# A hybrid decoder layer: later work on the decay rows, and transposes set one to three steps apart

## The chip, the cores and the metric

The kernel runs on one core of a Trainium2 chip. The metric is device time in microseconds (us): before the change the median of three runs is 1289.85 us (1289.18 to 1289.87).

## The reference, cut to what matters

One decoder layer works on 1024 prompt tokens and 32 sample tokens (8 sequences of 4). One input projection feeds two groups of heads, a gated delta rule (4 heads of width 128, chunks of tokens) and sliding-window attention; their outputs are joined, projected, normalised, sent through a SwiGLU block and normalised again. The change touches the delta rule and the keys of the attention:

```python
decay = jnp.exp(jnp.where(causal, gc[..., :, None] - gc[..., None, :], -jnp.inf))
A = jnp.where(strict, jnp.einsum('bnhid,bnhjd->bnhij', kb, kc) * decay, 0.0)
M = A + jnp.eye(C, dtype=A.dtype)
sol = lax.linalg.triangular_solve(M, rhs, left_side=True, lower=True, unit_diagonal=True)
u, w = sol[..., :DV], sol[..., DV:]
...
v_new = u_n - jnp.einsum('bhcd,bhde->bhce', w_n, S)
S = S * gl_n[..., None, None] + jnp.einsum('bhcd,bhce->bhde', kd_n, v_new)
```

## The kernel before, in words

Everything is stored transposed: features lie on the 128 partitions, tokens run along the free axis. The tokens are worked in two parts, s = 0 (tokens 0 to 511) and s = 1 (tokens 512 to 1023 and the 32 sample tokens, 544 columns). For each part `mix_in` (L1452) runs 22 dense tiles of the input projection: 4 for the keys of the delta heads, one for the attention keys (`kb`), one for the values, 4 for the attention queries, 4 each for the delta queries and values, 4 for the gates. A dense product (L426) is three float32r matmuls for each of 8 input blocks (high and low halves of both factors). For s = 0 it runs on 512 columns at once, for s = 1 in two groups of 272. Its weights are split on ScalarE (L162) and VectorE (L163). After both parts comes the output projection, `out_proj(0)` on 512 columns and `out_proj(1)` on two groups of 272, then the normalisation and the SwiGLU block.

All work beside the dense products is written as Python generators: `decay`, `delta_k`, `keys`, `attn`, `inverse`, `recur`, `sample_delta` and others. The program writes dense matmuls, and after every half tile it runs one round (`unit`, L422, and `pump`, L287) over the list of living generators, in the order in which they were started; each advances to its next `yield`. A yield carries a cost in ns of TensorE time, and a round ends when the sum reaches a budget of 2750 (3000 in the output projection). A round is called a step here. `idle(n)` (L321) lets n steps pass. A few generators (`sample_attn`, `sample_delta`) also advance in short rounds between.

That order is not yet the order on the engines. The program is built with `schedule_with_timeline_sim=True` (L2092): at build time each engine's queue is filled from the instructions that the builder takes to be ready at that time, the one written first going first; splits of weights and evacuations of dense products (`high_priority`) go ahead of all. So an instruction whose inputs are taken to be there can move ahead of its place when its engine has nothing else, and one that is written later loses its place to others that are ready. Dense matmuls are nearly always ready, so on TensorE a step's work stays at its step.

The steps of the second part are numbered here from the one in which the four `decay(1, h)` issue their loads (step 0). Every group of 272 columns ends one step: the key tile of head 3 ends with step 1, `kb` with 3, `vb` with 5, the attention queries with 7, 9, 11 and 13, the delta queries with 15 to 21, the values with 23 to 29, the gates with 31, 33, 35 and 37. The 8 tiles of `out_proj(0)` take two steps each, 38 to 53. Counted through the code, the generators that the change touches stand so:

- `decay(s, h)` (L586) loads a head's rows of decays and of beta from DRAM to all partitions (L598, L601), rests 9 steps (L603), adds a mask (L604, step 9), takes the exponential (L608, step 10) and multiplies (L610, step 11).
- `delta_k(s, h)` (L650) transposes the keys and forms their products in two PSUM banks (L662, L664); it squares the keys on ScalarE (L668), whose last one frees the first bank; the second is held until the decay rows are ready (L674 to L679). There are four such banks (tag `ms`). Heads 0 to 2 hold three of them from their transposes to step 11, and head 3, which needs two, makes its transposes then, in step 11, and is done in step 12.
- `inverse(s)` (L706) starts when all four heads are done (step 12). It moves 32x32 blocks to DRAM and back (L714, L717), inverts 64 of them at once by a loop of 31 columns on GpSimd (L726, L728, written until step 20), moves them back (L732, L739), rests 4 steps (L743), transposes three blocks on VectorE (L746, step 24) and then joins blocks by small matmuls: L754 and L755 in step 25, L765 to L768 in 26, L783 in 27, L797 in 28.
- `keys(s)` (L974) for s = 1 copies the sample keys on GpSimd (L987), waits one yield, and transposes keys (L992, L993) in step 7.
- `delta_w` (L847) needs the inverse: L852 and L857, from step 29 on. `recur(1)` (L867) needs all of it: four chunks of two steps each (L887 to L892, L904 and L906), steps 33 to 40, then the output transposes L947 in 42 and 43. `sample_delta` transposes the sample tokens' output (L1396) after that, in step 45, and adds the state products (L1427). `gate` (L1160) multiplies with the gates, and `split_mix` (L1771) splits the result, which `out_proj(1)` needs.

For s = 0 a step is half a tile of 512 columns, and the same generators run alike.

Of the kernel before, what the change touches and what calls it, by code (L numbers as in the profile page):

```python
# [87 lines left out]
IDLE = (9, 4, 2, 3, 2, 4)  # L88
# [120 lines left out]
def _program(k):  # L209
# [14 lines left out]
    def page(shape, dt, name, tag="hp"):  # L224
        assert room(tag), (tag, name)
        live[tag] += 1
        t = (k.fp if tag == "xp" else k.hp).tile([shape[0], HW_], dt, tag=tag, bufs=cap[tag], name=name)
        w = int(np.prod(shape[1:]))
        G.memset(t[:, 0:1].bitcast(F32), 0.0)
        v = t[:, :w]  # L230
        return v if len(shape) == 2 else v.rearrange("p (a b) -> p a b", b=shape[2])
# [15 lines left out]
    def bank(tag="ms"):  # L247
        assert room(tag)
        live[tag] += 1
        return k.pa.tile([P, 512], F32, tag=tag, bufs=cap[tag], name=tag)  # L250
# [6 lines left out]
    def drop(tag="hp", n=1):  # L257
        live[tag] -= n
        assert live[tag] >= 0
# [4 lines left out]
    def small(shape, name, bufs=1, dt=F32):  # L264
        return k.sp.tile(shape, dt, tag=name, bufs=bufs, name=name)
# [4 lines left out]
    def bc(ap, shape):  # L270
        return ap.broadcast_to(shape)
# [41 lines left out]
    def wait(*names):  # L313
        while not all(n in flags for n in names):
            yield BLOCK

    def have(tag, n=1):
        while not room(tag, n):
            yield BLOCK

    def idle(n):  # L321
        for _ in range(n):
            yield 0.0
# [262 lines left out]
    def decay(s, h):  # L586

        yield from wait(("g", s))
        if s:
            yield from wait(("E", 0))  # L590
        yield from have("hp")
        if s not in Bm:
            Bm[s] = small([P, 16, P], "Ball")
        Ball = Bm[s]
        g = gat[s]
        R = page([P, 4, P], F32, f"R{s}{h}")
        gd = g["dram"]
        dma(out=R.rearrange("p n t -> p (n t)"),  # L598
            in_=gd[h * 4:h * 4 + 4, :].rearrange("n t -> (n t)").partition_broadcast(P))
        RB = Ball[:, h * 4:h * 4 + 4, :]  # L600
        dma(out=RB.rearrange("p n t -> p (n t)"),  # L601
            in_=gd[16 + h * 4:16 + h * 4 + 4, :].rearrange("n t -> (n t)").partition_broadcast(P))
        yield from idle(IDLE[0])  # L603
        V.tensor_tensor(R, R, bc(C["rmask"].unsqueeze(1), [P, 4, P]), ALU.add)  # L604
        yield 0.0
        for n in range(4):
            c = h * 4 + n
            A.activation(R[:, n, :], R[:, n, :], AF.Exp, bias=g["ngc"][:, c:c + 1])  # L608
        yield 0.0
        V.tensor_tensor(RB, RB, R, ALU.mult)  # L610
        Rt[s, h] = R
        flags.add(("R", s, h))
        yield 0.0
# [92 lines left out]
    def inverse(s):  # L706
# [37 lines left out]
        for q in range(3):  # L744
            o = 32 * (q % 2)
            V.transpose(Dl[32 * q:32 * q + 32, :, o:o + 32], Eall[32 * q:32 * q + 32, :, 32 * q:32 * q + 32])  # L746
        yield 0.0
        yield from have("ms")
        yield from have("hp")
# [224 lines left out]
    def keys(s, kb):  # L974
        yield from have("hp", 4)
        kh = [page([P, 512], F32R, f"kh{s}{i}") for i in range(2)]
        kl = [page([P, 512], F32R, f"kl{s}{i}") for i in range(2)]
        for i in range(2):
            a, o = slice(64 * i, 64 * i + 64), slice(64 - 64 * i, 128 - 64 * i)
            A.copy(kh[i][a, :], kb[a, 0:512])  # L980
            A.copy(kh[i][o, :], kb[a, 0:512])
            V.tensor_tensor(kl[i][a, :], kb[a, 0:512], kh[i][a, :].bitcast(F32), ALU.subtract)
            V.tensor_tensor(kl[i][o, :], kb[a, 0:512], kh[i][a, :].bitcast(F32), ALU.subtract)
            yield 0.0
        at[s, "k"] = (kh, kl)
        if s:
            G.tensor_copy(ksT, kb[:, 512:544])  # L987
            yield 0.0
            yield from have("ms")
            yield from have("hp")  # L990
            pt = bank()
            tr(pt[:, 0:P], kb[:, 384:512], ident)  # L992
            tr(pt[0:32, P:2 * P], kb[:, 512:544], ident)  # L993
            kp = page([P, 2, P], F32, "kp")
            V.tensor_copy(kp[:, 0, :], pt[:, 0:P])
            V.tensor_copy(kp[0:32, 1, :], pt[0:32, P:2 * P])
            drop("ms")
            dma(out=O["k_p"], in_=kp[:, 0, :])
            dma(out=O["k_s"][:, 124:128, :], in_=kp[0:32, 1, :])
            drop()  # L1000
            dma(out=O["k_s"][:, 0:124, :], in_=I["cache_k"][:, 4:128, :])
            dma(out=O["v_s"][:, 0:124, :], in_=I["cache_v"][:, 4:128, :])
        drop()
        flags.add(("keys", s))
        yield 300.0
# [446 lines left out]
    def mix_in(s, before_last):  # L1452
# [6 lines left out]
        for h in range(4):  # L1459
            spawn(decay(s, h))  # L1460
        spawn(delta_k(s, 0, pre))
        for h in range(1, 4):
            spawn(delta_k(s, h, conv_dense(s, h, 4 + h)))
        spawn(norms_k(s))
        spawn(inverse(s))
        spawn(keys(s, kv_dense(s, 12, "kb")))
        spawn(vals(s, kv_dense(s, 13, "vb")))
        for m in range(4):
# [635 lines left out]
```

## Time and profile before

| | us |
|---|---|
| median of 3 runs | 1289.85 |
| the profiled execution: device time | 1288.69 |
| its span, first to last instruction | 1286.8 |
| TensorE (PE) busy | 1248.8 |
| VectorE (DVE) busy | 871.9 |
| ScalarE (ACT) busy | 616.2 |
| GpSimd (POOL) busy | 395.9 |

Times in the profile are us from the start of the span. A row of the timeline gives the start, the duration, engine, line, operation, what is written and read, the shape and how many follow each other; in square brackets, how long the engine had been idle before, and what ended that. PE is the matmuls and PEld the loads of their weights. A matmul's duration runs past the start of the next one, so the distance of two starts is its price. SP issues the transfers.

### The profile page before, as it was taken

Reading aid. Unit: us, or ns where it says so; the run is one execution under the profiler, and the core shown is the slowest. Engines: PE = TensorE matmul, PEld = TensorE weight load, DVE = VectorE, ACT = ScalarE, POOL = GpSimd, SP = SyncE. Lnnn points to the kernel's source line nnn. Section 1 sums busy time; section 2 is a strip of 40 time slices with the busy share of each in tenths; the row PEclk is TensorE's granted clock in tenths of the full one; section 3 lists DMA queues with packets and bytes.
Section 4 is the critical chain, followed back from the end, with each engine's and each line's share of the span. In section 5 each row is a group of like instructions: output and inputs, shape, how many; then the busy total and the mean of one; then the engine's idle time right before and its main releaser. Section 6 shows DMA issues by size and latency. Waiting matters only on the chain.

```text
span 1286.8 us, 24943 instructions
## 1 busy us (share of the span) xinstructions
PE 1248.8 (97%) x8701; PEld 1127.1 (88%) x8701; DVE 871.9 (68%) x1873; ACT 616.2 (48%) x1374; POOL 395.9 (31%) x1207
## 2 busy tenths in 40 slices
PE   9998999999999999996999999999999999999996
PEld 7887789999989888985999999999999998888995
DVE  6696975788885679868956655555655765622674
ACT  7674744757746433686322222322324554522453
POOL 1009411205722144437633433222332112201210
PEclk9999999999999999998999999999999999999999
DMA  7432341332133646444444422222324886733461
GB/s 252 138 90 70 93 133 39 104 120 83 45 116 105 193 140 205 157 155 155 167 155 141 147 92 74 76 83 75 112 86 119 295 269 190 214 100 114 143 218 47
DMA packets 119102, 170.81 MB, mean 133 GB/s; under 512 B 20272, under 2 KB 50096, under 8 KB 118960
## 3 DMA queue, kind: packets, MB, share of 16 engines
q1 hardware_dynamic: 118976, 169.22, 41.7%
q8 instruction: 68, 1.11, 0.3%
q14 instruction: 58, 0.48, 0.1%
HBM read 138.44 MB, written 31.75 MB: 132 GB/s over the span
## 4 chain that ended last, share of the span: by engine, by line
PE 48%; DVE 2%; DMA 1%; ACT 0%; issue 0%; DVEq 0%; SPq 0%; ACTq 0%; POOL 0%; POOLq 0%
PE acc L1990 6%; PE acc L1988 6%; PE acc L1989 6%; PE acc L1821 5%; PE acc L1819 5%; PE acc L1820 5%; PE ms L1819 5%; PE ms L1821 5%; PE ms L1820 5%; DMA hr<-hd 1%; DVE y L1554 1%; DVE wl L163 0%; PE ms L1522 0%; DMA wr<-in_w_ffo_t 0%; PE ms L1497 0%
## 5 line engine op out<-in xcount | busy, mean ns | idle before, releaser
L163 DVE TENSOR_TENSOR wl<-wr,wh 128x512 fp32r<-128x512 f32 x330 | 238.1, 725 | 141.0 <-ACT wh L162 131.6
L162 ACT CAST wh<-wr 128x512 fp32r<-128x512 f32 x330 | 197.2, 602 | 266.4 <-PE acc L1989 104.3
L433 PE MATMUL acc<-xh,wh 128*128 128x272 f32 (+1 forms) x528 | 174.5, 330 | 0.6 <-ACT qsm L1045 0.4
L434 PE MATMUL acc<-xl,wh 128*128 128x272 f32 (+1 forms) x528 | 173.7, 329 | 0.5 <-DVE xl L347 0.5
L435 PE MATMUL acc<-xh,wl 128*128 128x272 f32 (+1 forms) x528 | 173.6, 329 | 0.2 <-DVE wl L163 0.2
L1990 PE MATMUL acc<-hx,wl 128*128 128x272 f32 (+1 forms) x528 | 171.5, 325 | 1.5 <-DVE wl L163 1.4
L1988 PE MATMUL acc<-hx,wh 128*128 128x272 f32 (+1 forms) x528 | 171.8, 326 | 0.0
L162 ACT CAST wh<-S 128x512 fp32r<-128x512 f32 x88 | 54.4, 619 | 148.8 <-PE acc L1820 89.7
L1990 PEld LDWEIGHTS acc<-hx,wl 128*128 128x128 f32 x528 | 99.2, 188 | 10.6 <-DVE wl L163 2.4
L434 PEld LDWEIGHTS acc<-xl,wh 128*128 128x128 f32 x528 | 100.4, 190 | 8.9 <-issue 2.4
L433 PEld LDWEIGHTS acc<-xh,wh 128*128 128x128 f32 x528 | 100.4, 190 | 8.5 <-issue 1.0
L435 PEld LDWEIGHTS acc<-xh,wl 128*128 128x128 f32 x528 | 100.4, 190 | 8.0 <-issue 1.0
L1988 PEld LDWEIGHTS acc<-hx,wh 128*128 128x128 f32 x528 | 99.2, 188 | 8.2 <-issue 0.2
L1989 PE MATMUL acc<-hx,wh 128*128 128x272 f32 x352 | 101.5, 288 | 0.2 <-DVE hx L1718 0.2
L163 DVE TENSOR_TENSOR wl<-S,wh 128x512 fp32r<-128x512 f32 x88 | 72.2, 823 | 37.7 <-ACT wh L162 34.9
L1989 PE MATMUL acc<-hy,wh 128*128 128x512 f32 x176 | 69.4, 394 | 0.0
L1989 PEld LDWEIGHTS acc<-hx,wh 128*128 128x128 f32 x352 | 66.7, 189 | 0.7 <-DVE hx L1718 0.4
L433 PE MATMUL acc<-mh,wh 128*128 128x272 f32 (+1 forms) x192 | 64.0, 333 | 0.0
L434 PE MATMUL acc<-ml,wh 128*128 128x272 f32 (+1 forms) x192 | 63.3, 330 | 0.0
L435 PE MATMUL acc<-mh,wl 128*128 128x272 f32 (+1 forms) x192 | 63.1, 329 | 0.0
L1717 ACT CAST hx<-hr 128x272 fp32r<-128x272 f32 (+1 forms) x66 | 31.7, 486 | 46.1 <-DMA hr<-hd 41.5
L1659 POOL TENSOR_TENSOR S<-wr,S 128x512 f32<-128x512 f32 x22 | 34.8, 1581 | 53.4 <-DVE wl L163 53.4
(631 smaller groups left out, 3481.0 us busy)
## 6 DMA issues: line engine op xcount, KB each, us to landing
wr<-in_w_ffo_t SPq DMA_DIRECT2D x120, 256.0 KB, 3.0
wr<-in_w_ffi_t SPq DMA_DIRECT2D x108, 256.0 KB, 2.7
wr<-in_w_in_t SPq DMA_DIRECT2D x88, 256.0 KB, 2.6
wr<-in_w_out_t SPq DMA_DIRECT2D x32, 256.0 KB, 3.3
hd<-x SPq DMA_DIRECT2D x22, 272.0 KB, 2.7
hr<-hd SPq DMA_DIRECT2D x44, 136.0 KB, 2.8
hd<-x SPq DMA_DIRECT2D x22, 256.0 KB, 2.0
hr<-hd SPq DMA_DIRECT2D x22, 256.0 KB, 5.1
```

The costliest lines, as they stand in the source:

```text
L162: nc.scalar.copy(hi, raw)
L163: nc.vector.tensor_tensor(lo, raw, hi.bitcast(F32), ALU.subtract)
L433: mm(ps[:, :cw], wh, xh[kt][:, c0:c0 + cw], start=(kt == 0), stop=False)
L434: mm(ps[:, :cw], wh, xl[kt][:, c0:c0 + cw], start=False, stop=False)
L435: mm(ps[:, :cw], wl, xh[kt][:, c0:c0 + cw], start=False, stop=(kt == n - 1))
L1659: G.tensor_tensor(t["S2"], W.get(r["A12"]), t["S2"], ALU.subtract)
L1819: mm(o, wh[:, kt, :], xh, start=(start and kt == 0), stop=False, **kw)
L1820: mm(o, wh[:, kt, :], xl, start=False, stop=False, **kw)
L1821: mm(o, wl[:, kt, :], xh, start=False, stop=(kt == 3), **kw)
L1988: mm(ps, wh[:, f % 4, :], xh, start=(f == 0), stop=False)
L1989: mm(ps, wh[:, f % 4, :], xl, start=False, stop=False)
L1990: mm(ps, wl[:, f % 4, :], xh, start=False, stop=(f == NF - 1))
```

## The change: what it does

```diff
@@ decay
-        yield from idle(IDLE[0])
+        yield from idle(IDLE[0] + 5 * s)
@@ inverse
             V.transpose(Dl[32 * q:32 * q + 32, :, o:o + 32], Eall[32 * q:32 * q + 32, :, 32 * q:32 * q + 32])
+            yield 0.0
         yield 0.0
@@ keys, for s = 1
             G.tensor_copy(ksT, kb[:, 512:544])
-            yield 0.0
+            yield from idle(3)
             yield from have("ms")
```

Three edits. In the second part the work on the decay rows rests 14 steps instead of 9. In both parts the three block transposes of the inverse stand in three steps instead of one, and with the yield that follows them the matmuls that use them come three steps later. In the second part the key transposes come two steps later. No instruction is added or taken away.

## The prediction, made before the change ran

> **What bounds the kernel now.** The page first: the sum over the engines says which of them can be late.
>
> ```profile
> span 1286.8 us, 24943 instructions
> PE 1248.8 (97%) x8701; PEld 1127.1 (88%) x8701; DVE 871.9 (68%) x1873; ACT 616.2 (48%) x1374; POOL 395.9 (31%) x1207
> ```
>
> TensorE is idle for 1286.8 - 1248.8 = 38 us. The edits add and remove no instruction, so they can only change this idle time and what follows from it. The waits of PE come next (who waited, for whom, us in total, times, longest):
>
> ```profile
> PE ms L992 <- ACT junk L668: 2.3, 1, 2.3
> PE ms L754 <- DVE hs L699: 2.0, 1, 2.0
> PE ms L1427 <- DVE S L1432: 1.5, 2, 0.9
> PE acc L433 <- ACT qsm L1045: 0.4, 1, 0.4
> PE ms L755 <- DVE Dl L746: 0.3, 1, 0.3
> ```
>
> Two of these stand at places the change touches: the key transpose L992 and the first joining product of the inverse, L754. Then the stretches around them (length, then busy us of PE, PEld, DVE, ACT, POOL, granted clock, DMA share, GB/s):
>
> ```profile
> 260.00:270.00 10.00, 7.73 (x51) 7.50 (x50) 7.32 (x18) 6.82 (x22) 0.10 (x1) 0.83 0.69 225
> 350.00:360.00 10.00, 8.05 (x107) 7.54 (x105) 9.21 (x26) 5.81 (x20) 0.20 (x2) 0.83 0.69 172
> 480.00:490.00 10.00, 8.53 (x68) 6.72 (x65) 10.00 (x18) 3.01 (x6) 4.38 (x14) 0.97 0.28 84
> 490.00:500.00 10.00, 10.00 (x66) 9.52 (x65) 9.27 (x25) 2.25 (x5) 3.62 (x42) 0.85 0.91 264
> ```
>
> Each wait costs twice: idle time (2.27 us in the first stretch, 1.95 in the second) and then a clock of 0.83 over the 10 us, about 0.17 x 10 = 1.7 us of lost speed. So each place holds about 3.7 to 4.0 us. The last two rows are the end of the second part, where the last state products hold up TensorE: 10 - 8.53 = 1.47 us and 0.18 x 10 = 1.8 us of clock.
>
> **Part 1, the key transposes two steps later.** TensorE's own order at the wait, then what VectorE and ScalarE did (rows of the timeline):
>
> ```profile
> 249.81 0.29 PE L435 MATMUL acc<-xh,wl 128*128 128x272 f32 x1
> 249.93 0.29 PE L433 MATMUL acc<-xh,wh 128*128 128x272 f32 x1
> ...
> 260.71 0.29 PE L433 MATMUL acc<-xh,wh 128*128 128x272 f32 x1
> 263.27 0.33 PE L992 MATMUL ms<-cst,kb 128*128 128x128 f32 x1 [2.27 <-ACT junk L668]
> ...
> 264.79 0.43 PE L433 MATMUL acc<-xh,wh 128*128 128x272 f32 x1
> ```
>
> ```profile
> 261.54 0.69 DVE L604 TENSOR_TENSOR R<-R,cst 128x512 f32<-128x512 f32 x1 [5.98 <-DMA R<-gd]
> 262.26 0.43 DVE L1042 SCALAR_TENSOR_TENSOR qs<-acc,qs 64x272 fp32r<-64x272 f32 x1
> ```
>
> ```profile
> 262.27 0.69 ACT L608 ACTIVATE R<-R,gt 128x128 f32<-128x128 f32 x2 [4.59 <-DVE R L604]
> 262.87 0.26 ACT L668 ACTIVATE junk<-ms 128x128 f32<-128x128 f32 x1
> ...
> 275.45 0.20 ACT L1045 ACTIVATE qsm<-acc 128x32 f32<-128x32 f32 x1 [1.06 <-DVE qs L1042]
> ```
>
> The chain reads backwards: L992 wants the bank that the last L668 frees; ScalarE has L608 in front of it, L608 waits for L604, and L604 holds VectorE for 5.98 us because the decay rows have not landed. A group of 24 matmuls, 0.12 us apart, is 3.0 us, so two steps are about 6 us: at 260.7 + 6 = 267 the bank has been free since 263.1 and L992 waits for nothing. The value transpose L1015, a step later than L992 was, meets it at 263.7. This wait goes.
>
> But VectorE and ScalarE stay where they are, and the first group's L1042, behind L604 in its queue, was held too. The evacuations of the first query tile end with L1045 at 275.45 + 0.20, and PE already waits for that one (0.4, the fourth row of the waits). If it arrives 3.7 us sooner, it waits that much longer there. So part 1 alone gives nothing. The bounds: -4.0 us if VectorE's order moves in its favour, +0.5 if the later wait slows the clock longer.
>
> **Part 2, five more steps before the decay work.** Does it move L604, which is the root?
>
> ```profile
> L598 SPq DMA_DIRECT2D R<-gd x8: 326/382/1179, 48.8 to 260.9; - x8
> L604 DVE TENSOR_TENSOR R<-R,cst x8: 669/692/693, 52.9 to 268.5; 128x512 f32<-128x512 f32 x8
> ```
>
> In the first part L604 starts 4.1 us after the first load was issued, although nine steps, each of 12 matmuls or at least 1.4 us, stand between them in the code. It has moved ahead to an idle VectorE, and more steps cannot hold what nine did not. So I keep the stall of 5.98 us and cost this edit at nothing here; were L604 held instead, part 1 would give its 4.0 us.
>
> What it does move is TensorE's work behind it. Heads 0 to 2 keep their banks, in the code's count, to step 16 instead of 11, so head 3's transposes go to step 16, the inverse starts in step 17 and not 12, its loop is written until step 25 and its rest lasts to 29. Attention of the first two heads gets its banks in step 16 too, one or two steps late, and is done before step 24, so nothing that ends the part waits for it.
>
> **Part 3, three steps for the block transposes.** With them L754 goes from step 25 to 33, and the later products from 26, 27, 28 to 34, 35, 36. What it waited for:
>
> ```profile
> 284.81 0.38 PE L664 MATMUL ms<-kT 128*128 128x128 f32 x2
> ```
>
> ```profile
> 297.10 1.12 DVE L677 SCALAR_TENSOR_TENSOR Ball<-ms,hs,Ball 128x128 f32<-128x128 f32 x4
> ...
> 355.26 0.70 DVE L746 STREAM_TRANSPOSE Dl<-Eall 32x512 f32<-32x512 f32 x1 [0.63 <-DMA Eall<-ed]
> ```
>
> ```profile
> 305.51 0.23 POOL L726 TENSOR_TENSOR itmp<-Db,Ab 64x31 f32<-64x31 f32 x1 [1.83 <-DMA Ab<-bd]
> ```
>
> ```profile
> 349.10 0.51 SPq L732 DMA_DIRECT2D ed<-Db  x1
> ```
>
> ```profile
> 356.02 0.24 PE L754 MATMUL ms<-Dl,Ball 32*32 32x32 f32 x2 [1.95 <-DVE hs L699]
> ...
> 358.46 0.26 PE L755 MATMUL ms<-Dl,Ball 32*32 32x32 f32 x1
> ```
>
> The data path is L664, L677 12.3 us later, the loop on GpSimd from 305.5 to 349.1, two transfers, L746. Five steps put L664 some 15 us later, and the data at most as much, since L677 and the loop find no more work in front of them: 355.3 + 15 = 370, the last transpose 2.2 us after. TensorE comes to L754 eight steps later, at least 8 x 3.0 = 24 us, at 378 or after. So it finds the data there with 6 us to spare. Gain: 1.95 of idle and, between 1.4 (8.05 of 10 us busy at a loss of 0.17) and 1.7, of clock; I take 3.5. For s = 0 the three steps take the 0.3 us of L755.
>
> At this place a rule can be weighed. The clock came down to 0.83 after pauses of 2.27 and 1.95 us, and a 272-column matmul took 0.43 us instead of 0.29 after the first. The Trainium skill, "TensorE: Matmul & The Clock Gate", section "What's actually happening", says that the array drops to half its clock after an idle window of about 3.4 us; by it pauses this short would cost no clock, and the edit would be worth 1.95 instead of 3.5. The rows disagree with it, and I go by the rows.
>
> **The price of it: a later end of the part.** All that needs the inverse moves: L857 to step 38, the recurrence to 39 to 46, L947 to 48 and 49, and L1396 behind them to 49. Step 53 is the last of `out_proj(0)`; after it nothing covers the chain.
>
> ```profile
> 397.29 1.06 PE L892 MATMUL ms<-S,mx 128*128 128x128 f32 x8
> ...
> 420.33 0.40 PE L435 MATMUL acc<-mh,wl 128*128 128x512 f32 x1
> ...
> 475.01 0.40 PE L434 MATMUL acc<-ml,wh 128*128 128x512 f32 x1
> 475.25 0.39 PE L435 MATMUL acc<-mh,wl 128*128 128x512 f32 x1
> 475.47 0.27 PE L1396 MATMUL ms<-cst,sov 128*128 128x128 f32 x1
> ...
> 488.97 0.50 PE L433 MATMUL acc<-mh,wh 128*128 128x512 f32 x1
> ```
>
> TensorE's work is the same, so without waits `out_proj(1)` could start at 488.97 - 1.47 - 3.8 (parts 2 and 3) = 483.7. The chain: two chunks of the recurrence (five groups like L892 each, at 0.8 to 1.06 us: 4.3) and L857 (four such groups, 4) leave the gates' stretch, so `out_proj(0)` starts at 420.3 - 3.8 - 12.6 = 404. From there to step 49 are 12 steps of 12 matmuls, 0.23 apart: 33 us. L857, four chunks and L947 are 4 + 17 + 2; the sample's work between I estimate at 10 from the same rows. So L1396 at 404 + 33 + 23 + 10 = 470. From L1396 to `out_proj(1)` it was 13.5 us, so 483.5 to 484: just in time. Were each of the three steps that the recurrence can slip by its own latency lost, 8.3 us more, 492. I take 486, nearer to the low end, because the sample's steps, which crowded chunks 2 and 3 before, are then past: 3.0 us sooner than before.
>
> **The sum.** -3.5 - 0.3 for the waits at the inverse, 0 for parts 1 and 2, and at the end 486 - 483.7 = 2.3 us of waiting where there were 1.47, +0.8: -3.0 us. The profiled execution took 1288.69, 1.9 above its span and 1.2 below the median; on the median 1289.85 - 3.0 = 1286.8. What follows `out_proj(1)` is written in the same order and I leave it.
>
> **The rivals.**
>
> (a) Both waits go: L604 gives way to the evacuations, and part 1 gives its 4.0. Against it speaks L604's own early start; for it, that five steps lower its claim further. 1286.8 - 4.0 = 1282.8.
>
> (b) The end takes over, slower than before. If the recurrence slips by its three steps, `out_proj(1)` starts at 492 instead of 488.97, 3.0 later, with a longer pause and its slow clock (1.7 as above): 1294.5. It decides as soon as L1396 starts later than 475.5. For it: 4 steps remain behind L1396 where there were 8. Against it: before, L1396 came late at its place too, 10 us of dense work from the end.
>
> (c) Nothing that can be measured: what is won at the inverse is lost to a new wait of its size, for instance at the banks that attention now gets later, or the change of order does not reach the engines. 1289.5.
>
> (d) The slow clock stays although the wait goes, which is what the skill's rule would make of it: 1289.85 - 1.95 - 0.3 + 0.8 (the end, as above) = 1288.4.
>
> **Chances.** A measurement of this kernel tells 0.2%, 2.6 us, from no change. Forecast 0.42, (a) 0.12, (b) 0.2, (c) 0.2, (d) 0.06. The forecast lies close to that bound, so I count 0.3 of its 0.42 as faster; with (a) that is 0.42. (c), (d) and the rest of the forecast are 0.38, (b) 0.2. The range goes from 1281.5, below (a), to 1294, into (b).
>
> **What would show it.** Right: no wait at L754 and L755, and a clock of 1.0 there; L992 without wait, but a longer one of PE for L1045 some 10 us on; L604 still idle for about 6 us before; L1396 between 468 and 476. Wrong: L754 waiting as before, no pause for L1045, or PE idle for more than 4 us ahead of `out_proj(1)`.

## The result and the profile after

The changed kernel takes 1293.74 us (median of 14 runs, 1290.99 to 1295.45), the kernel before 1289.94 beside it (14 runs). The ratio is 1.0028, with a 95% interval of 1.0017 to 1.0039: slower by 3.6 us, 2.2 to 5.0. The forecast was 3 us faster; the time lies inside the range given, near its upper end.

The profiled execution took 1292.28 us, 1.5 under the median. In the changed kernel, lines behind L746 stand one number higher (L992 is L993, L1396 is L1397). The page's sums, against 1248.8 of PE, 871.9 of DVE and 395.9 of POOL before:

```profile
span 1290.5 us, 24956 instructions
PE 1249.7 (97%) x8701; PEld 1127.5 (87%) x8701; DVE 869.3 (67%) x1873; ACT 611.9 (47%) x1370; POOL 395.1 (31%) x1207
```

TensorE is idle for 40.8 us, 2.8 more than before, and busy for 0.9 more. Its waits in the second part (who waited, for whom, us in total, times, longest):

```profile
PE acc L435 <- DVE wl L163: 2.4, 1, 2.4
PE ms L1024 <- DVE Ball L677: 2.4, 1, 2.4
PE ms L993 <- DVE Ball L677: 1.6, 1, 1.6
...
PE ms L1134 <- DVE vb L843: 0.7, 1, 0.7
...
PE ms L841 <- ACT vT L644: 0.5, 1, 0.5
```

The wait at L754 is gone. Four of these five are new or as good as new (the first, for a split of weights, was 0.15 us before). L992 waits less, but the transpose of the sample values, L1024, now waits 2.35 us for L677, the instruction that frees the PSUM banks of the keys. The same stretches as in the prediction (length, busy us of PE, PEld, DVE, ACT, POOL, granted clock, DMA share, GB/s), with the ten us behind the first of them, and the one where L754 stands now:

```profile
260.00:270.00 10.00, 8.36 (x65) 7.78 (x63) 7.21 (x16) 6.32 (x19) 0.10 (x1) 1.00 0.57 208
270.00:280.00 10.00, 7.70 (x39) 7.70 (x40) 9.62 (x30) 3.97 (x11) 0.20 (x2) 0.66 0.30 85
350.00:360.00 10.00, 7.61 (x63) 7.40 (x62) 9.93 (x23) 9.97 (x35) 8.67 (x20) 1.00 0.18 54
480.00:490.00 10.00, 9.82 (x71) 7.51 (x70) 9.28 (x16) 5.62 (x13) 8.60 (x24) 1.00 0.16 55
490.00:500.00 10.00, 9.08 (x70) 7.97 (x71) 10.00 (x32) 0.68 (x2) 2.01 (x16) 1.00 0.71 210
380.00:400.00 20.00, 19.79 (x313) 18.55 (x314) 15.04 (x47) 11.15 (x24) 3.73 (x25) 1.00 0.47 156
```

At 270 to 280 TensorE was busy for 9.56 us before, at full clock; part of the pauses around the key transposes has moved there, and 3.4 us of clock are lost, twice as much as before. At 350 to 360 TensorE still stands for 2.4 of 10 us, though L754 is no longer there, and GpSimd is busy for 8.67 us where it had been for 0.20: the loop of the inverse has moved in. Its first column and the transfer behind its last, and the start of L604, by the timeline:

```profile
316.34 0.67 POOL L726 TENSOR_TENSOR itmp<-Db,Ab 64x31 f32<-64x31 f32 x1 [3.24 <-DMA Ab<-bd]
359.60 0.51 SPq L732 DMA_DIRECT2D ed<-Db  x1
261.76 0.69 DVE L604 TENSOR_TENSOR R<-R,cst 128x512 f32<-128x512 f32 x1 [7.16 <-DMA R<-gd]
386.09 0.21 PE L755 MATMUL ms<-Dl,Ball 32*32 32x32 f32 x1
479.55 0.27 PE L1397 MATMUL ms<-cst,sov 128*128 128x128 f32 x1
490.91 0.39 PE L433 MATMUL acc<-mh,wh 128*128 128x272 f32 x1
```

The loop runs at 316.3 to 359.6, where it ran at 305.5 to 349.1; L604 did not move (261.54 before). The last two rows are L1396 and the first matmul of `out_proj(1)`.

What TensorE waited for at 355.78 stands in VectorE's order ahead of it:

```profile
350.62 4.50 DVE L1107 TENSOR_SCALAR st<-st,ast 128x256 f32<-128x256 f32 x8
355.04 1.55 DVE L163 TENSOR_TENSOR wl<-wr,wh 128x512 fp32r<-128x512 f32 x2
```

Eight scalings of the softmax take 4.50 us, 0.56 each; the weight split comes behind them. Those at 300 to 400, 24 for the kernel before and then 20 for the changed one (ns: least, median, most):

```profile
L1106 DVE TENSOR_SCALAR st<-st,ast x24: 345/352/676, 300.5 to 352.9; 128x256 f32<-128x256 f32 x24
```

```profile
L1107 DVE TENSOR_SCALAR st<-st,ast x20: 337/451/974, 299.7 to 360.2; 128x256 f32<-128x256 f32 x20
```

Sorted by whether they start while the loop runs, they take 0.35 us outside it and 0.64 inside (8 of 32) before the change, 0.35 and 0.57 (15 of 32) after it.

**The balance** to the end of `out_proj(1)`, whose last matmul starts at 541.1 before and 543.4 after. Both kernels issue the same 4165 matmuls up to there. Three stretches, of the kernel before and then of the changed one:

```profile
240.00:300.00 60.00, 56.22 (x444) 55.36 (x443) 46.93 (x141) 41.11 (x135) 9.43 (x31) 0.97 0.35 114
300.00:400.00 100.00, 97.11 (x983) 91.34 (x982) 79.38 (x195) 58.17 (x155) 54.79 (x144) 0.98 0.29 84
470.00:500.00 30.00, 28.53 (x190) 24.28 (x189) 25.63 (x58) 9.33 (x20) 13.50 (x60) 0.94 0.48 143
```

```profile
240.00:300.00 60.00, 56.06 (x433) 55.28 (x432) 45.06 (x127) 40.56 (x127) 8.21 (x30) 0.94 0.34 112
300.00:400.00 100.00, 96.17 (x969) 90.51 (x968) 83.65 (x217) 59.67 (x168) 54.36 (x141) 1.00 0.33 96
470.00:500.00 30.00, 28.90 (x192) 23.90 (x191) 25.99 (x57) 12.26 (x24) 13.00 (x48) 1.00 0.38 115
```

Idle time is the length less the busy time of PE, lost clock the length times what the clock lacks of 1 (summed from stretches of 2 us). Idle and clock together: 0 to 240 +0.7; 240 to 300 +1.9 (the clock); 300 to 400 -0.8; 400 to 470 -0.1; 470 to the end -2.1. That is -0.3, against +2.3 measured. The other 2.6 us TensorE is busy at full clock: the same matmuls in another order. The traces show where most of it is. Counted from each start to the next, without idle time and lost clock, the products of the recurrence (L887 to L892, L904, L906) and those of the sample tokens with the states (L1427, L1447) take 41.1 us before and 43.9 after; the dense products give 0.7 of it back. In the two kernels without the loop's instructions (the last pair below) the sums are again 41.1 and 43.9, and the dense products give back 0.4. So the loop has no share in this price of the new order.

What follows `out_proj(1)` is written the same in every kernel and took 745.7 and 747.0 us in these two traces, and 745.2 to 749.5 over all traces of this study, so one trace cannot place a difference of 3.6 us to the last microsecond; the comparisons below are of medians.

### The profile page after: what moved, and what is told of

Same layout as the page of the kernel before. It is cut to its first block, busy times and chain, and to the rows that moved or that the text cites. A ratio compares the mean times of both kernels' runs of the same rounds, so it can differ in the third digit from the quotient of the medians.

```text
span 1290.5 us, 24956 instructions
## 1 busy us (share of the span) xinstructions
PE 1249.7 (97%) x8701; PEld 1127.5 (87%) x8701; DVE 869.3 (67%) x1873; ACT 611.9 (47%) x1370; POOL 395.1 (31%) x1207
## 4 chain that ended last, share of the span: by engine, by line
PE 44%; DMA 2%; DVE 2%; issue 1%; ACT 1%; POOL 0%; DVEq 0%; SPq 0%; ACTq 0%; POOLq 0%
PE acc L1991 5%; PE acc L1989 5%; PE acc L1990 5%; PE acc L1820 5%; PE acc L1822 5%; PE acc L1821 5%; PE ms L1822 5%; PE ms L1820 5%; PE ms L1821 5%; DMA hr<-hd 2%; DVE y L1555 1%; DVE wl L163 1%; ACT hx L1718 0%; PE ms L1523 0%; DMA wr<-in_w_ffo_t 0%
## 5 line engine op out<-in xcount | busy, mean ns | idle before, releaser
L163 DVE TENSOR_TENSOR wl<-wr,wh 128x512 fp32r<-128x512 f32 x330 | 241.3, 735 | 136.7 <-ACT wh L162 130.6
L435 PE MATMUL acc<-xh,wl 128*128 128x272 f32 (+1 forms) x528 | 172.8, 328 | 2.4 <-DVE wl L163 2.4
L435 PEld LDWEIGHTS acc<-xh,wl 128*128 128x128 f32 x528 | 100.1, 190 | 9.5 <-DVE wl L163 2.6
L435 PE MATMUL acc<-mh,wl 128*128 128x272 f32 (+1 forms) x192 | 62.5, 325 | 0.0
L1820 PE MATMUL ms<-B22h,wh 128*128 128x272 f32 x176 | 50.7, 288 | 0.3 <-DVE x L1955 0.3
```

The lines of the kernel that those rows point to most:

```text
L163: nc.vector.tensor_tensor(lo, raw, hi.bitcast(F32), ALU.subtract)
L435: mm(ps[:, :cw], wl, xh[kt][:, c0:c0 + cw], start=False, stop=(kt == n - 1))
L1820: mm(o, wh[:, kt, :], xh, start=(start and kt == 0), stop=False, **kw)
```

## The experiments

Two theories at first. **T** (L in later runs; in two runs split into its halves, banks and loop): what comes later in the middle costs, through new waits. **E**: the late end costs, the prediction's rival (b).

### Each edit alone, and the pairs

The decay edit alone (7 runs):

```diff
-        yield from idle(IDLE[0])
+        yield from idle(IDLE[0] + 5 * s)
```

> Only the decay edit (14 steps instead of 9, second part). Theory T (the loss comes with the later decay: head 3's products, the banks it frees and the loop on GpSimd all come some 10 us later, and TensorE waits at new places, the key transposes and the weights at 355): slower than the kernel before by 2 to 4 us, most of the change's 3.8. Theory E (the loss is the late end of the part, rival b of the prediction): the matmuls on the transposed blocks stand at step 30 instead of 33, so L1396 comes at about 476 and the time is within 1.5 us of before. The forecast's own view would be 3 us faster, as the wait at L754 goes.

Measured: ratio 1.0054 (1.0035 to 1.0074), 7 us slower. L1396 came at 485.6, not 476, and TensorE waited 1.9 us for a weight split, as in the changed kernel, and 3.5 us at L1015 for L677, which frees the banks. L604 was not moved by five steps, nor was it by two fewer in a later run; that one is the second fence:

```profile
261.18 0.69 DVE L604 TENSOR_TENSOR R<-R,cst 128x512 f32<-128x512 f32 x1 [6.12 <-DMA R<-gd]
```

```profile
261.52 0.69 DVE L604 TENSOR_TENSOR R<-R,cst 128x512 f32<-128x512 f32 x1 [6.30 <-DMA R<-gd]
```

So the edit costs by what it moves behind the decay rows, not at them. The yields in the inverse alone (12 runs):

```diff
             V.transpose(Dl[32 * q:32 * q + 32, :, o:o + 32], Eall[32 * q:32 * q + 32, :, 32 * q:32 * q + 32])
+            yield 0.0
```

> Only the yields in the inverse, for both parts. Theory T: nothing moves at the decay rows; L754 comes three steps later (some 9 us, 365) than its data (355.3), so its wait of 1.95 us goes, and the time is 0 to 3 us less than before. Theory E: whatever the inverse gives is lost at the end: L1396 goes from 475.5 to about 478, time 0 to 2 us more than before.

Measured: 0.9990 (0.9977 to 1.0003). L754 no longer waits, L1396 came at 474.2; no price at the end, no clear gain. The later keys alone (12 runs):

```diff
-            yield 0.0
+            yield from idle(3)
```

> Only the key transposes two steps later (second part). Both theories: L992 no longer waits 2.27 us, but the evacuation that the matmuls wait for moves no sooner than 275.4, so PE waits there instead: within 1 us of before.

Measured: 0.9998 (0.9985 to 1.0011). The wait of 2.27 us came back as six shorter ones between 263 and 277, 4.65 us in all, and the same 1.7 us of clock was lost, ten us later; the forecast of nothing holds, but the wait for L1045 that was to replace it is only 0.53 of them. The pairs, the first two of these diffs and then the first and the third:

> The decay edit and the inverse's yields, without the later keys. Decay alone cost 7 us, all three edits 3.8, so some 3 us come back from the others. If they come from the inverse's yields (alone 1.3 us faster, within the error), this run is at 3 to 5 us over before; if from the keys' place behind the later banks, it is at 6 to 8. End theory: L1396 comes still later than with the decay edit alone, 7 us or more.

> The decay edit and the later keys, without the inverse's yields: the other half of the pair. If the 3 us come from the keys, 3 to 5 us over before; if from the inverse's yields, 6 to 8. End theory: as with the decay edit alone, L1396 at about 485 and 7 us.

Measured: 1.0062 (1.0044 to 1.0080, 8 runs) and 1.0052 (1.0036 to 1.0068, 10 runs). Neither pair gives back what all three do together (1.0028; the second pair's interval reaches that of the three), so the edits do not add up as forecast, and the runs do not say which of them softens the decay edit. What holds the decay edit is slower.

### The end

The decay edit with the tail of the inverse brought forward:

```diff
-        yield from idle(IDLE[0])
+        yield from idle(IDLE[0] + 5 * s)
...
-        yield from idle(IDLE[1])
+        yield from idle(IDLE[1] - 3 * s)
```

> The decay edit, but the inverse rests 1 step instead of 4 before its block transposes in the second part, and no new yields: the matmuls on the blocks stand at step 27 (33 in the changed kernel, 25 before), with their data at about 366 just in time. Theory E (late end): the end of the part is as before (L1396 at 474 to 476), so the time is at or under that of before, by 0 to 3 us. Theory T: the later decay keeps its price whatever the inverse does behind it: 2 to 4 us slower than before.

Measured: 1.0049 (1.0035 to 1.0063, 10 runs), as slow as the decay edit alone. But L1396 came at 479.7, not at 474 to 476, and TensorE waited 2.7 us at L754 for its blocks, so this run does not decide between the theories. Then the tail, or the inverse as a whole, held back in the kernel before:

```diff
         yield from wait(*[("K", s, h) for h in range(4)])
+        yield from idle(5 * s)
```

> The kernel before, with the inverse alone starting 5 steps later in the second part; the decay rows, the products of the keys and their PSUM banks are left as before. The decay edit alone cost 0.54% (7 us). Three theories of that cost. Banks (heads 0 to 2 hold three of four banks 5 steps longer, so attention's work is pushed together): this run leaves the banks alone, so within 1.5 us of before. Loop (the loop on GpSimd now runs beside other VectorE work, whose operations it slows, so weights come late at about 355): 3 to 7 us slower. End (L1396 and the sample's products slip into the start of out_proj(1)): L1396 at 479 to 486 and 3 to 7 us slower.

```diff
-        yield from idle(IDLE[1])
+        yield from idle(IDLE[1] + 5 * s)
```

> The kernel before, with 5 more steps between the inverse's transfers and its block transposes in the second part: the loop on GpSimd stays at 305 to 349, the banks stay, L754 comes in step 30 as with the decay edit alone. Banks: within 1.5 us of before, or faster by the 3 us of L754's wait. Loop: the same. End: 3 to 7 us slower, as with the decay edit alone, with L1396 at 479 to 486.

Measured: 1.0099 (1.0069 to 1.0130, 4 runs) and 1.0082 (1.0055 to 1.0108, 5 runs): E's price is real, and larger than I had it. But the first of the two was not the experiment it was meant to be. Its loop started at 307.3, against 305.5 before: the build moved it ahead of its five steps, as it does with L604, so both runs hold back the tail alone. What that costs (10.6 us by the ratio, 11.6 by the medians), in the second run: the last matmul of `out_proj(0)`, then L1396, and the 15 us behind it.

```profile
484.40 0.40 PE L435 MATMUL acc<-mh,wl 128*128 128x512 f32 x1
488.96 0.45 PE L1396 MATMUL ms<-cst,sov 128*128 128x128 f32 x1 [4.16 <-DVE sov L1389]
```

```profile
490.00:505.00 15.00, 15.00 (x83) 13.82 (x82) 12.36 (x37) 2.94 (x7) 5.98 (x11) 0.50 0.31 91
```

L1396 comes behind the last dense matmul, TensorE stands for 4.16 us, and then all of it runs at half the clock, 10.2 us lost by stretches of 2 us. Is this what the changed kernel pays? Its L1397 comes 9.7 us ahead of the last matmul of `out_proj(0)`, and its rows at 470 to 500 show 1.10 us of idle time and no lost clock. The test is the changed kernel with its tail 4 steps sooner:

```diff
-        yield from idle(IDLE[1])
+        yield from idle(IDLE[1] - 4 * s)
```

> The changed kernel, but the inverse of the second part rests no step (4 before) ahead of its block transposes, so that L754 stands in step 29 instead of 33 (25 before), 2 steps behind its data. Theory E (what the change loses, it loses because the inverse's products, the recurrence and the sample's output come late; resting 5 steps more in the tail alone cost 11.6 us): the end is nearly as before, the waits at the inverse stay away, so 1 to 3 us faster than before. Theory L (the loss comes with the later banks and the later loop on GpSimd, whatever the tail does): still 3 to 5 us slower.

Measured: 1.0032 (1.0019 to 1.0045, 12 runs), the changed kernel's own time. The output transposes came 7 us sooner (467.5 instead of 474.4), L1396 itself later (487.4, since the sample's own chain came late), and TensorE neither stood nor slowed from 470 to the end of `out_proj(1)`. The end is free here and the loss stays: E falls for the changed kernel. The same time is not made up in the same places, though: this kernel lost 5.1 us of clock at 240 to 300 and stood for 2.1 us at 400 to 470, where the changed kernel lost 3.4 and did not stand.

### The first part, and the other sign

The changed kernel, with the inverse's yields in the second part alone:

```diff
-            yield 0.0
+            if s:
+                yield 0.0
```

> The changed kernel, with the inverse's yields in the second part alone. In the traces the first part lost 1 to 1.7 us between 100 and 200 with these yields and won 1.3 at 240 to 260. Both theories: within 1.5 us of the changed kernel, 2.5 to 5 us over before; if the first part's yields have a net price, it is nearer to 2.5.

Measured: 1.0036 (1.0020 to 1.0052, 12 runs): the first part has no share in the loss that shows. Then the decay rows two steps sooner in the kernel before, and the same with L754 held at its step:

```diff
-        yield from idle(IDLE[0])
+        yield from idle(IDLE[0] - 2 * s)
...
-        yield from idle(IDLE[1])
+        yield from idle(IDLE[1] + 2 * s)
```

> The kernel before with the opposite sign: the decay rows of the second part rest 7 steps instead of 9, and everything behind them comes two steps sooner, L754 to step 23. Theory E: L1396 comes some 5 us sooner (470), out_proj(1) starts without its pauses and slow clock: 1 to 4 us faster. Theory L: the order beside the loop and the banks is again another; a change of either sign within 2 us. A price of its own: the exponentials on ScalarE stand sooner in front of the evacuations of the keys.

> As before with the decay rows 2 steps sooner, but the inverse rests 2 steps more before its block transposes, so that L754 stands in step 25 as in the kernel before, with its data some 4 us sooner. Theory E: the end is as before; the wait of 1.95 us at L754 and its slow clock go, 0 to 3.5 us faster. Against the run with the tail sooner it shows which of the two is worth more, the data ahead of L754 or the end.

Measured: 1.0036 (1.0020 to 1.0052) and 1.0045 (1.0030 to 1.0060), 12 runs each. Sooner is slower too, which neither theory had said. In the first of them the loop starts at 290.3, and TensorE waits at 315 for a copy on VectorE:

```profile
314.98 1.12 PE L1121 MATMUL ms<-cst,st 128*128 128x128 f32 x4 [3.85 <-DVE ptS L1125]
```

Sorted by the start of the loop, all kernels of the study whose tail is not simply held back and whose loop is whole:

| loop starts | kernel | ratio |
|---|---|---|
| 290.3, 291.4 | decay sooner; with L754 held | 1.0036, 1.0045 |
| 299.0 | L604 kept in order (below) | 1.0006 |
| 304.5 to 306.7 | inverse's yields; before; keys | 0.9990, 1, 0.9998 |
| 309.9 to 318.7 | with the decay edit, seven kernels | 1.0028 to 1.0062 |
| 325.6 | changed, L604 kept in order (below) | 1.0069 |

The kernel before has its loop where it is cheap. But heads, banks and loop move together in this table, so it is no proof.

### Making the edit reach the decay rows

`pin` keeps an instruction in program order on its engine, so that the build cannot float it:

```diff
-        V.tensor_tensor(R, R, bc(C["rmask"].unsqueeze(1), [P, 4, P]), ALU.add)
+        m = V.tensor_tensor(R, R, bc(C["rmask"].unsqueeze(1), [P, 4, P]), ALU.add)
+        if s:
+            pin(m)
```

> The kernel before, with L604 of the second part kept in program order on VectorE, so that it can't be moved ahead of its step (9). Theory P (the pause of VectorE at L604, 6 us, is what holds up the evacuations of keys and queries behind it, and with them TensorE at 260 to 276): VectorE no longer stands still at 255 to 261, the waits of TensorE at 260 to 280 shrink, 1 to 4 us faster. Theory L (loop and banks): nothing changes there; within 1.5 us of before.

> The changed kernel, with L604 of the second part kept in program order, step 14: now the edit reaches the work that it names. Theory P: L604 starts near 277 instead of 262 and without a pause; the waits at the key transposes go, and the run is 3 to 5 us faster than the changed kernel, at the time of before or under it. Theory L: the pause goes, but loop and banks are as late as in the changed kernel or later: at most 1.5 us faster than it.

Measured: 1.0006 (0.9993 to 1.0019) and 1.0069 (1.0052 to 1.0086, 6 runs). In the second, VectorE and ScalarE do what theory P said; L604, and L1045 of the first query tile (here L1048), which came at 275.5 before:

```profile
280.04 2.49 DVE L604 TENSOR_TENSOR R<-R,cst 128x512 f32<-128x512 f32 x4
```

```profile
262.14 0.20 ACT L1048 ACTIVATE qsm<-acc 128x32 f32<-128x32 f32 x1 [0.47 <-DVE qs L1045]
```

```profile
240.00:300.00 60.00, 60.00 (x492) 59.67 (x491) 45.75 (x119) 40.55 (x117) 8.13 (x29) 1.00 0.39 129
300.00:400.00 100.00, 91.93 (x895) 84.99 (x893) 80.03 (x211) 62.95 (x180) 52.58 (x148) 0.98 0.27 80
```

The stretch to 300 is perfect: no idle time, full clock, 5.5 us better than before. The next 100 us give back 5.2, 8.07 of idle instead of 2.89, with the loop at 325.6 to 385.7, and up to the end of `out_proj(1)` TensorE is busy at full clock for 4.2 us more. The kernel is slower than either theory said: taking the waits at the key transposes away does not decide the time.

### The loop

Without the loop and its steps, in both kernels; the blocks of the inverse in the second part are left as unit matrices:

```diff
-        for c in range(31):
+        for c in range(0 if s else 31):
```

> The kernel before without the loop of 31 columns on GpSimd in the second part (the blocks of its inverse are left as unit matrices), everything else in place. It is the partner of the next run. VectorE's scaling of the softmax takes 0.35 us per operation throughout instead of 0.57 to 0.64 beside the loop. Theory L: 1 to 3 us faster than before. Otherwise within 1 us.

> The changed kernel without the loop on GpSimd in the second part (its blocks are left as unit matrices). Theory L (the loop's place beside VectorE's work is what costs): the distance to the kernel before without the loop is under 1.5 us, where it is 3.8 with the loop. If the distance stays at 3 to 5 us, the loop is not the cause and the later banks and products are.

Measured: 1.0010 (0.9995 to 1.0025) and 0.9984 (0.9971 to 0.9997), 12 runs each. The kernel before gains nothing, where L had said 1 to 3 us. The changed kernel becomes the faster one, but with the loop's seven yields gone the tails are seven steps sooner too. So the steps back, and only the instructions out:

```diff
         for c in range(31):
+            if s:
+                if c % 4 == 3:
+                    yield 0.0
+                continue
             tmp = small([64, 256], "itmp", 1)
```

> The kernel before without the instructions of the loop on GpSimd in the second part, but with its steps, so that L754 stays in step 25 (the blocks of its inverse are left as unit matrices). It is the partner of the next run. Theory L: the wait at L754 goes and VectorE is not slowed, 1 to 4 us faster than before. Theory of the tail's place: the same gain of 2 to 3.5 us for the wait.

> The changed kernel without the loop's instructions, but with its steps, so that L754 stays in step 33 (its blocks are left as unit matrices). Theory L (the loop's work beside VectorE makes the loss): 1286 to 1289.5, some 4 to 6 us faster than the changed kernel and within 1.5 us of its partner. If the place of the tail made the gain of the run without loop and steps: 1292 to 1295, as the changed kernel, and 3 us or more over its partner.

Measured: 0.9960 (0.9948 to 0.9972) and 0.9963 (0.9950 to 0.9975), 6 runs each. The distance between the two kernels, 0.28% with the loop, is 0.03% without it, with every step in its place: 0.4 us by the means, and with six runs each an interval of 2.1 us either way, against 3.6 us, 2.2 to 5.0. The loop's instructions are worth some 5 us in the kernel before and 8 in the changed one. The kernel before gained these 5 us only with the seven steps back, so the steps have a price of the same size. Their stretches at 300 to 400, the kernel before first, and VectorE's order ahead of the weight split in the changed one:

```profile
300.00:400.00 100.00, 99.09 (x1027) 93.03 (x1026) 71.92 (x198) 60.44 (x160) 18.98 (x83) 1.00 0.29 88
```

```profile
300.00:400.00 100.00, 99.78 (x1021) 94.97 (x1020) 80.31 (x226) 62.97 (x174) 19.15 (x96) 1.00 0.36 109
```

```profile
347.98 2.18 DVE L1111 TENSOR_SCALAR st<-st,ast 128x256 f32<-128x256 f32 x8
350.08 1.28 DVE L163 TENSOR_TENSOR wl<-wr,wh 128x512 fp32r<-128x512 f32 x2
```

The eight scalings take 2.18 us instead of 4.50, and TensorE's idle time in this stretch is 0.22 instead of 3.83: the waits at L435, L841 and L1134 are gone. The two at the banks, L993 and L1024, are still there (1.8 and 2.35 us), so they are not what separates the kernels. But the pair takes away the old wait with the new ones: without the loop's instructions the blocks are there at 308.7 in the kernel before, and L754 waits for nothing. At 300 to 400 the change is then 0.7 us better (0.91 against 0.22 of idle), as it is 0.8 better with the loop. So the pair shows that the loop's instructions make these waits, and that the distance hangs on them; that the distance lies in this stretch it does not show.

## Why the prediction was wrong, point by point

**The step that failed** is in part 3: the gain of 3.5 taken whole, with nothing for what the moved loop runs beside. "L677 and the loop find no more work in front of them" held: the loop came 10.8 us later and the blocks at 365.7, under the bound of 370. The loop was a link of a chain to me, with a start and an end. It is also 43 us of work on GpSimd that slows VectorE beside it. Before, it ended at 349 and the last eight scalings of the softmax stood behind it; from 316 to 360 it covers both of the last groups, and the weight splits between them. At 300 to 400 the change took away 2.89 us of idle time and 1.7 of clock, as forecast at L754 and a little more, and 3.83 of idle came in their place: -0.8 instead of -3.5. That the loop's instructions make the waits at L435, L841 and L1134, and that the distance of the kernels hangs on them, is shown by the last pair. By which way is only argued: VectorE's slower operations are measured, but pages of the main buffer are claimed by a small write on GpSimd (L229), which queues behind the loop as well, and VectorE waited for such a claim for up to 3.9 us in the changed kernel, 4.5 with the decay edit alone and 2.9 before.

**A second step failed, as large as the first:** "TensorE's work is the same", in the price of the end. The matmuls are the same 4165, but in the new order they keep TensorE busy for 2.6 us more at full clock, most of it at the products of the recurrence and of the sample tokens, with the loop's instructions and without them. Why these products take longer in that order stays open.

The whole sum of the two traces is then: -0.3 for waits and clock, where the forecast had -3.0, 2.6 for the order, and 1.3 behind `out_proj(1)`, which lies inside the spread of that stretch.

**Part 1, nothing.** Right about the chain: L604 idle for 7.16 us, L1045 still at 275.5, and alone the edit moves nothing. Wrong about the new wait: not L1045 but L677, through the banks that the decay edit holds longer, which the sum left out: the clock lost 1.7 us more at 240 to 300. The size of that is one trace's: with the inverse's yields in the second part alone this stretch lost 1.7 us of clock, and with the tail 4 steps sooner 5.1.

**Part 2, L604 does not move.** Right in every trace in which it is not pinned, with 7, 9 and 14 steps: it starts at 259.9 to 264.7. Costing the edit at nothing there was right for L604 and wrong for what stands behind it: alone it costs 7 us.

**Part 3, no wait at L754 and full clock.** Right: data at 368.4, L755 at 386.1, clock 1.00.

**The end.** L1396 was to come at 470 and came at 479.55, `out_proj(1)` at 490.9 instead of 486. The row at 488.97 that the prediction takes for its start before has 512 columns and is still of `out_proj(0)`; the first with 272 stood at 489.98, so it came 0.9 us later. The price was to be +0.8 and was -2.1: the state products ran with less waiting and at full clock. Rival (b) gave 1294.5 and its point, 475.5, was passed, so its time nearly came out, by another cause than its own. Where it does act, with the tail held back, it costs 10.6 us; I had its pause and clock at 4.7, with 1.7 for the clock, which was 10.2.

**Rivals (a), (c) and (d).** (a) fell: L604 did not give way, and part 1 gave nothing. (c), a new wait of the size of the old one, for instance through attention's banks, is the nearest to what happened; it gave too little because it stopped at one wait. (d) fell: with the wait at L754 gone, the clock stood at 1.00 there.

## What to carry to other kernels

Before moving a step, look at what the moved work runs beside at its new place, above all a long loop on an engine that slows another; price the loop's neighbours, not only its two ends. The same matmuls in another order need not take the same time. A rest in the program text is no rest on the engine where a build may float instructions: see in the trace whether the named instruction moved, and if not, cost the edit by what did. And a rival whose number comes out is not yet the cause: bring its mechanism forward, as with the tail here, and see whether the time follows.

## What the runs showed of the hardware

VectorE's scaling of 128x256 floats takes 0.35 us alone and 0.57 to 0.64 us while GpSimd runs the loop. The products with a PSUM input (L824) take 0.34 us with the loop and without it. The Trainium skill, "SBUF — State Buffer", section "Who interferes with whom", says that VectorE and GpSimd share one pair of ports, for which such scalings can contend, while an instruction with at most one input in SBUF, outside VectorE's two-port modes, stays clear of it; both agree with these rows.

The clock needs no pause to fall. With the decay edit alone, TensorE was busy throughout (length, then PE):

```profile
486.00:490.00 4.00, 4.00 (x39) 3.35 (x38) 2.76 (x9) 2.67 (x8) 3.69 (x3) 1.00 0.20 70
492.00:500.00 8.00, 8.00 (x34) 7.30 (x34) 8.00 (x24) 1.19 (x2) 2.01 (x11) 0.50 0.68 200
```

What came before is 48 of the small state products (32 rows) with six dense matmuls between them. A pause of 2.39 us, at 355.78 in the changed kernel, left the clock at 1.00. Up to the end of `out_proj(1)` the clock lost in one stretch is 0, 1.7, 3.4, 5.1 or 10.2 us in the traces, multiples of one half of 3.4 us. The Trainium skill, "TensorE: Matmul & The Clock Gate", section "What's actually happening", has a free-running window of about 3.4 us that sets half the clock when idle: the length agrees, but here the half clock also followed pauses of 2 us and, without any pause, the small matmuls.
